# Four first products by quarters beside the modulation, and their loads on another queue

## The chip, the core and the metric

The program runs on one core of a Trainium2 chip, in one launch. A core has a matrix engine (TensorE, here PE, with its weight loads as PEld), a vector engine (VectorE, DVE), a scalar engine (ScalarE, ACT), GpSimd (POOL) and a sync engine (SP) that does little but issue transfers. The metric is the device time of one execution in microseconds; lower is better. The time before is 2888.81 us, the median of three runs (2887.84 to 2892.58).

## The reference

The model is one inference step of a two-layer backbone over 128 context tokens and 128 latent tokens of width 2048, all in float32. Each layer does, for both groups of tokens with the same weights:

```
sh1, sc1, g1, sh2, sc2, g2 = silu(cond) @ ada_w + ada_b        # six vectors of 2048: the modulation
h = rmsnorm(x, nw0) * (1 + sc1) + sh1
u = h @ w_in            # columns: q, k, v | hyena | r, k, v of RWKV | low-rank decay and rate (w_dn, a_dn) | gate
o = concat(attention, hyena, rwkv) @ w_out
x = x + g1 * rmsnorm(o, nw1)
h = rmsnorm(x, nw2) * (1 + sc2) + sh2
x = x + g2 * rmsnorm(relu(h @ w1)^2 @ w2, nw3)
```

The first product of a layer, `h @ w_in`, needs `sc1` and `sh1`, and these need two sixths of `ada_w`: 33.6 MB of the layer's 100 MB of modulation weights. RWKV is a recurrence over the tokens in both directions; the kernel does it in blocks, with a triangular inverse on the vector engine.

## The kernel before

All products with big weights are done in two parts: a weight tile is loaded as float32 (`wr`, up to 512 KB), the scalar engine rounds it to its high part (`wh`, L232), the vector engine subtracts to get the low part (`wl`, L233), and the matrix engine adds three products: high by high, high by low, low by high (L508, L511, L512 in `ws`; L530, L533, L534 in `as_`). The activations (`acth`, `actl`) are split in the same way by `norm` (L468 to L491), in four chunks of 512 of the 2048 model columns. A chunk is four tiles of 128 of the contraction, so a product can begin on the first chunk before the rest is normalised.

The modulation of layer 0 is the boot. Its shift and scale are done in eight groups, one for each of four chunks and the two vectors (`ada_group`, L334). A group loads eight tiles of 512 KB and multiplies them by silu(cond); its 16 matmuls of 512 columns are 32 instructions in the trace. A group ends with a copy (L353) and small products that turn rows into columns (L357). Two groups run in turn (`ada_boot`, L420). After both groups of a chunk `norm` makes that chunk of the activations.

Weight tiles stand in rings: `wr` has four buffers (`raw=4`), `wa` six (`araw=6`). The groups take `wr` and `wa` by turns, the products take `wr`; all of these loads are issued by SP in one order (L342 and L231). A load into a ring waits until the buffer's last reader is done, and what SP has queued behind it waits too.

`mixer_first` (L1120) starts two products of layer 0, `wa` (the low-rank columns, four blocks of 96) and RWKV's `k` (three blocks of 128). In the boot loop of `build` (L1319) each chunk of `norm` is followed by four contraction tiles of the one and four of the other. Both add up in the two PSUM tiles tagged `mm` (`mm_bufs=2`), so these two are taken through the boot. `mixer` (L1127) then does the gate's product (L1155), and RWKV's `r` and `v` (L1158), and only then puts the recurrence of RWKV (`rwkv_batch`) in the list of side work (L1159). Side work is small work on all engines that `run` (L1109) lays between products at a given rate; the modulation vectors still to come (`ada_vector`, L374) are laid between them in the same way. In layer 1 the mixer has the same order, with no boot.

The instructions of an engine are put in order by a scheduler that works on its own model of durations, so their order can differ from the order of the code.

Of the kernel before, what the change touches and what calls it, by code (L numbers as in the profile page):

```python
# [9 lines left out]
F32 = mybir.dt.float32  # L10
# [8 lines left out]
KT = 16  # L19
# [14 lines left out]
def _shape_constants():  # L34
# [56 lines left out]
    for k, v in c.items():  # L91
# [18 lines left out]
            ni=3, w2=0.5, w3=3, w4=2, w5=0.4, fill=16, b1=2, b2=5)  # L110
# [47 lines left out]
class Kern:  # L158
# [65 lines left out]
    def wload(self, src, nk, ncol):  # L224

        nc = self.nc
# [4 lines left out]
        nc.sync.dma_start(v(raw), src.rearrange("(k p) c -> p k c", p=128))  # L231
# [102 lines left out]
    def ada_group(self, l, P, i, cg):  # L334

        nc, sb, A = self.nc, self.sb, self.A
        ps = self.sm()
        c0 = i * D + cg * 512
        for kq in range(8):
            tag = ("wr", "wa")[kq // 2 % 2]  # L340
# [153 lines left out]
    def ws(self, act, w, widths, ps):  # L494
# [4 lines left out]
        for kq in range(KT // nk):  # L499
            hi, lo = self.wload(w[kq * nk * 128:(kq + 1) * nk * 128, :], nk, ncol)  # L500
            for kk in range(nk):
                k = kq * nk + kk
                hh, hl = act[k // 4][0][:, k % 4, :], act[k // 4][1][:, k % 4, :]
                c0 = 0
                for b, wd in enumerate(widths):
                    o = ps[0:wd, b * 256:(b + 1) * 256]
                    h, lw = hi[:, kk, c0:c0 + wd], lo[:, kk, c0:c0 + wd]
                    m = self.product(nc.tensor.matmul(o, lhsT=h, rhs=hh, start=(k == 0 and b % 2 == 0), stop=False, skip_group_check=True))  # L508
# [3 lines left out]
                    nc.tensor.matmul(o, lhsT=lw, rhs=hh, start=False, stop=(k == KT - 1), skip_group_check=True)  # L512
# [596 lines left out]
    def run(self, gen, side=0, ada=0.0):  # L1109

        for n in gen:
            n /= 6144
# [190 lines left out]
    def build(self):  # L1303
# [8 lines left out]
        n, cg, todo = 0, 0, deque()  # L1312

        def products():
            for _, g in first:
                for _ in range(4):
                    next(g)

        while self.adaq or todo:  # L1319
            if self.adaq:  # L1320
                self.ada_boot()
# [7 lines left out]
            if cg < 4 and len(self.adaq) < 2 * (4 - cg) - 1:  # L1329

                todo.append((n + self.o["b1"], lambda: next(norm)))
                todo.append((n + self.o["b2"], products))
                cg += 1
# [58 lines left out]
```

## Time and profile before

| what | us |
|---|---|
| median of three runs | 2888.81 |
| the profiled execution's own time | 2894.91 |
| its span, first to last instruction | 2893.1 |
| PE busy | 2810.1 (97%) |
| DVE busy | 1646.9 (57%) |
| ACT busy | 1232.4 (43%) |
| POOL busy | 179.4 (6%) |
| bytes moved, mean rate | 654.56 MB, 226 GB/s |

The profiled execution is 6.1 us above the median. Matmuls overlap in the array and their ends are modelled, so a busy PE is not PE at its peak: the pace of products is better read from the starts of successive matmuls than from the busy time. The share of DMA can read slightly over 1.

### The profile page before, as it was taken

To read this page: it belongs to the slowest core of one execution; us is meant where nothing else is said; L and a number is where in the kernel's file an instruction comes from. 1 tells how busy PE (TensorE), PEld (TensorE's weight loads), DVE (VectorE), ACT (ScalarE), POOL (GpSimd) and SP (SyncE) were. 2 spreads that over 40 slices of the span, in tenths; PEclk is the share of its full clock that TensorE was granted. 3 is DMA by queue.
4 is the path that set the end of the run, shared out by engine and by line. 5 is a ranking of instruction groups with operands and counts; after the bars stand their busy time and mean duration, and the time that the engine had idled before them with its cause. 6 is when DMAs were issued, how large, how long until landed. Compare 5 with 4: busy or idle time off the path is not lost. (4 is left out here: it accounts for less than half of the span.)

```text
span 2893.1 us, 47892 instructions
## 1 busy us (share of the span) xinstructions
PE 2810.1 (97%) x19163; PEld 2306.6 (80%) x19163; DVE 1646.9 (57%) x2635; ACT 1232.4 (43%) x1878; POOL 179.4 (6%) x368
## 2 busy tenths in 40 slices
PE   6899999999999999999998999999989999999998
PEld 3586888766797897897876979877669989899896
DVE  1356766777544454444455577677675545555555
ACT  2254445434544343343345454453354444444343
POOL 0012101202000000000000111011010000000000
PEclk8999999999999999999999999999899999999999
DMA  9985675478888787887876746534686666666674
GB/s 333 333 300 201 223 231 161 152 261 285 311 268 268 261 270 256 272 274 262 288 279 210 210 149 193 168 111 142 200 297 184 184 186 185 189 189 183 190 241 150
DMA packets 326185, 654.56 MB, mean 226 GB/s; under 512 B 48709, under 2 KB 86158, under 8 KB 325835
## 3 DMA queue, kind: packets, MB, share of 16 engines
q1 hardware_dynamic: 311456, 610.88, 65.3%
q0 software_dynamic: 12928, 36.98, 3.9%
q10 hardware_dynamic: 1579, 3.64, 0.3%
q8 instruction: 150, 2.46, 0.3%
q14 instruction: 72, 0.59, 0.1%
HBM read 632.21 MB, written 19.20 MB: 225 GB/s over the span
## 5 line engine op out<-in xcount | busy, mean ns | idle before, releaser
L233 DVE TENSOR_TENSOR wl<-wr,wh 128x1024 fp32r<-128x1024 f32 (+2 forms) x792 | 929.0, 1175 | 921.1 <-ACT wh L232 909.6
L232 ACT CAST wh<-wr 128x1024 fp32r<-128x1024 f32 (+2 forms) x792 | 798.7, 1010 | 1175.5 <-PE mm L511 522.6
L508 PE MATMUL mm<-acth,wh 128*128 128x256 f32 (+1 forms) x3200 | 921.2, 288 | 6.5 <-ACT acth L489 4.6
L511 PE MATMUL mm<-actl,wh 128*128 128x256 f32 (+1 forms) x3200 | 904.7, 283 | 0.0
L512 PE MATMUL mm<-acth,wl 128*128 128x256 f32 (+1 forms) x3200 | 902.9, 282 | 1.9 <-DVE wl L233 1.9
L508 PEld LDWEIGHTS mm<-acth,wh 128*128 128x128 f32 (+1 forms) x3200 | 601.8, 188 | 59.2 <-issue 32.1
L512 PEld LDWEIGHTS mm<-acth,wl 128*128 128x128 f32 (+1 forms) x3200 | 602.8, 188 | 7.3 <-DVE wl L233 4.3
L511 PEld LDWEIGHTS mm<-actl,wh 128*128 128x128 f32 (+1 forms) x3200 | 600.9, 188 | 4.5 <-issue 3.3
L530 PE MATMUL mm<-wh,fh 128*128 128x512 f32 x1024 | 404.9, 395 | 0.0
L533 PE MATMUL mm<-wl,fh 128*128 128x512 f32 x1024 | 403.3, 394 | 1.0 <-DVE wl L233 0.9
L534 PE MATMUL mm<-wh,fl 128*128 128x512 f32 x1024 | 401.6, 392 | 0.0
L530 PEld LDWEIGHTS mm<-wh,fh 128*128 128x128 f32 x1024 | 192.2, 188 | 56.6 <-issue 8.4
L533 PEld LDWEIGHTS mm<-wl,fh 128*128 128x128 f32 x1024 | 192.2, 188 | 44.9 <-DVE wl L233 2.7
L534 PEld LDWEIGHTS mm<-wh,fl 128*128 128x128 f32 x1024 | 192.0, 187 | 45.2
L387 PE MATMUL ada<-wa,cs 128*32 128x512 f32 x1280 | 193.3, 609 | 8.4 <-DMA wa<-in_ada_w_dram 8.4
L530 PE MATMUL mm<-wh,osh 128*128 128x512 f32 x256 | 106.9, 418 | 0.7 <-ACT osh L1192 0.7
L387 PEld LDWEIGHTS ada<-wa,cs 128*32 128x32 f32 x1280 | 36.6, 109 | 85.9 <-issue 53.6
L533 PE MATMUL mm<-wl,osh 128*128 128x512 f32 x256 | 103.1, 403 | 1.5 <-DVE wl L233 1.5
L534 PE MATMUL mm<-wh,osl 128*128 128x512 f32 x256 | 102.8, 402 | 0.0
L921 PE MATMUL sm<-rZR,rKB 64*128 64x256 f32 x384 | 75.1, 424 | 1.0 <-DVE rLA L925 1.0
L530 PE MATMUL mm<-wh,acth 128*128 128x512 f32 (+1 forms) x192 | 74.3, 387 | 0.0
L533 PE MATMUL mm<-wl,acth 128*128 128x512 f32 (+1 forms) x192 | 68.8, 358 | 0.0
(323 smaller groups left out, 2565.4 us busy)
## 6 DMA issues: line engine op xcount, KB each, us to landing
wr<-in_mlp_w_dram SPq DMA_DIRECT2D x512, 512.0 KB
wa<-in_ada_w_dram SPq DMA_DIRECT2D x352, 512.0 KB
wr<-in_w_in_dram SPq DMA_DIRECT2D x96, 512.0 KB
wr<-in_w_in_dram SPq DMA_DIRECT2D x112, 384.0 KB
wr<-in_w_out_dram SPq DMA_DIRECT2D x56, 512.0 KB
wr<-in_ada_w_dram SPq DMA_DIRECT2D x32, 512.0 KB
gb<-gate POOLq DMA_DIRECT2D x16, 512.0 KB, 8.7
xd<-acc SPq DMA_DIRECT2D x24, 256.0 KB
```

The costliest lines, as they stand in the source:

```text
L232: nc.scalar.copy(hi, raw)
L233: nc.vector.tensor_sub(lo, raw, hi)
L387: nc.tensor.matmul(ps[32 * j:32 * j + 32, :], lhsT=self.cs[:, kk, :], rhs=w[2 * (kk - k + 1) + j // 2][:, 512 * (j % 2):512 * (j % 2) + 51 ...
L508: m = self.product(nc.tensor.matmul(o, lhsT=h, rhs=hh, start=(k == 0 and b % 2 == 0), stop=False, skip_group_check=True))
L511: nc.tensor.matmul(o, lhsT=h, rhs=hl, start=False, stop=False, skip_group_check=True)
L512: nc.tensor.matmul(o, lhsT=lw, rhs=hh, start=False, stop=(k == KT - 1), skip_group_check=True)
L530: m = self.product(nc.tensor.matmul(o, lhsT=hh, rhs=hi[:, kk, :], start=first, stop=False))
L533: nc.tensor.matmul(o, lhsT=hh, rhs=lo[:, kk, :], start=False, stop=False)
L534: nc.tensor.matmul(o, lhsT=hl, rhs=hi[:, kk, :], start=False, stop=last)
L921: self.beside(nc.tensor.matmul(ps[h][:, i * 256:(i + 1) * 256], lhsT=KB[hs, d, g, i, :], rhs=ZR[hs, d, g, :, :].rearrange("p i t -> p (i t ...
```

## The change

1. `mixer_first` is now one generator. It goes through the four chunks of the contraction, and in each through four products: `wa`, `k`, `r` and `v`. Each quarter of a product takes a PSUM tile of its own, and is then copied (first chunk, ACT) or added (later chunks, DVE) to a float32 tile in SBUF (`F`). `ws` takes the range of contraction tiles, `ks`.
2. The loads of these 32 weight tiles are issued by GpSimd (`q=nc.gpsimd`), not by SP.
3. In `ada_group` only the first chunk's groups use the `wr` ring; the later ones use `wa` alone (L340).
4. The boot loop lays 1.2 steps of the modulation (`bo`) beside each contraction tile of the products, for the next chunk's groups.
5. In `mixer` layer 0 finishes the last chunk, takes the convolutions from `F`, adds the recurrence to the side work, and then does the gate's product. Layer 1 does `wa`, then `k`, `r`, `v`, then adds the recurrence, then the gate.

```diff
-            tag = ("wr", "wa")[kq // 2 % 2]
+            tag = "wa" if cg > 0 else ("wr", "wa")[kq // 2 % 2]
...
-        nc.sync.dma_start(v(raw), src.rearrange("(k p) c -> p k c", p=128))
+        (q or nc.sync).dma_start(v(raw), src.rearrange("(k p) c -> p k c", p=128))
...
     def mixer_first(self, l, act):
 
+
+        nc, sb = self.nc, self.sb
         W = self.A["w_in"][l]
-        ps = self.mm(), self.mm()
-        return [(ps[0], self.ws(act, W[:, C_WA:C_WA + 384], [96] * 4, ps[0])),
-                (ps[1], self.ws(act, W[:, C_R + 768:C_R + 768 + 384], [128] * 3, ps[1]))]
+        F = self.F = {n: sb([128, 1024], F32, tag="f" + n) for n in ("wa", "k", "r", "v")}
+        cols = {"wa": (C_WA, [96] * 4), "k": (C_R + 768, [128] * 3), "r": (C_R, [128] * 3), "v": (C_R + 1536, [128] * 3)}
+        for c in range(4):
+            for n, (c0, widths) in cols.items():
+                ps = self.mm()
+                yield from self.ws(act, W[:, c0:c0 + sum(widths)], widths, ps, range(4 * c, 4 * c + 4), nc.gpsimd)
+                dst, src = (x[0:widths[0], 0:256 * len(widths)] for x in (F[n], ps))
+                if c == 0:
+                    nc.scalar.copy(dst, src)
+                else:
+                    nc.vector.tensor_add(dst, dst, src)
+            yield None
...
-        self.run(first[0][1], 1, ada)
-        self.rwkv_lora(first[0][0], P)
-        self.run(first[1][1], 1, ada)
-        rkv_conv("k", 0, first[1][0])
+        if first is not None:
+
+            self.run(first, 1, ada)
+            self.rwkv_lora(self.F["wa"], P)
+            for nm in "krv":
+                rkv_conv(nm, 0, self.F[nm])
+        else:
+            ps = self.mm()
+            self.run(self.ws(act, W[:, C_WA:C_WA + 384], [96] * 4, ps), 1, ada)
+            self.rwkv_lora(ps, P)
+            rkv(0)
+        self.side.add(self.rwkv_batch(l, P, 0, u), self.rwkv_out(l, P, 0), self.rwkv_batch(l, P, 1, u), self.rwkv_out(l, P, 1))
         ps = self.mm()
         self.run(self.ws(act, W[:, C_G:C_G + 256], [128] * 2, ps), o["sh"], ada)
         self.rwkv_gate(ps, P)
-
-        rkv(0, "rv")
-        self.side.add(self.rwkv_batch(l, P, 0, u), self.rwkv_out(l, P, 0), self.rwkv_batch(l, P, 1, u), self.rwkv_out(l, P, 1))
...
+        for c in range(4):
+
+            next(norm)
+            if c < 3:
+                left, due = 2 * (2 - c), 0.0
+                for step in iter(lambda: next(first), None):
+                    due += self.o["bo"]
+                    while due >= 1 and len(self.adaq) > left:
+                        self.ada_boot()
+                        due -= 1
+                while len(self.adaq) > left:
+                    self.ada_boot()
```

What this does to the order, at three places. The first is PE at the end of the second chunk's groups, before: `sm_245` and `sm_248` are the groups' sums, `sm_475` and `sm_478` those of the next chunk, `sm_489` and `sm_503` the transposed activations, `mm_111` is `wa`.

```order
L357 MATMUL sm_245<-const_66,arow_459 128x2 x4
L348 MATMUL sm_248<-wa_453,cs_71 32x512 x2
L357 MATMUL sm_248<-const_66,arow_461 128x2 x4
L348 MATMUL sm_475<-wr_476,cs_71 32x512 x2
L479 MATMUL sm_489<-const_66,xn_487 128x128 x4
L479 MATMUL sm_503<-const_66,xn_501 128x128 x4
L348 MATMUL sm_475<-wr_481,cs_71 32x512 x2
L348 MATMUL sm_478<-wr_479,cs_71 32x512 x2
L348 MATMUL sm_478<-wr_515,cs_71 32x512 x2
L348 MATMUL sm_475<-wa_521,cs_71 32x512 x2
L348 MATMUL sm_478<-wa_523,cs_71 32x512 x2
L508 MATMUL mm_111<-acth_105,wh_526 96x256
```

The same place now; `mm_509` is the quarter of `v`, `sm_243` and `sm_309` are the groups' sums.

```order
L512 MATMUL mm_509<-acth_103,wl_544 128x256
L357 MATMUL sm_243<-const_66,arow_540 128x2 x4
L357 MATMUL sm_309<-const_66,arow_557 128x2 x4
L479 MATMUL sm_586<-const_66,xn_584 128x128 x4
L479 MATMUL sm_600<-const_66,xn_598 128x128 x4
L348 MATMUL sm_581<-wa_582,cs_71 32x512 x2
L348 MATMUL sm_581<-wa_646,cs_71 32x512 x2
L348 MATMUL sm_631<-wa_632,cs_71 32x512 x2
L348 MATMUL sm_631<-wa_670,cs_71 32x512 x2
L348 MATMUL sm_581<-wa_688,cs_71 32x512 x2
L348 MATMUL sm_631<-wa_707,cs_71 32x512
L508 MATMUL mm_612<-acth_105,wh_614 96x256
```

The groups' last matmuls have moved among the products of the chunk before, and the products now stand right ahead of the small products of L357; what lies between L357 and the next chunk's first product has stayed much the same. The second place is the loads: SP before, at the first chunk's products.

```order
L231 DMA wr_367<-in_w_in_dram 128x2x384
L231 DMA wr_391<-in_w_in_dram 128x2x384
L342 DMA wa_415<-in_ada_w_dram 128x2x512
L342 DMA wa_421<-in_ada_w_dram 128x2x512
L342 DMA wr_427<-in_ada_w_dram 128x2x512
L342 DMA wr_429<-in_ada_w_dram 128x2x512
```

POOL now, from its beginning, with what each load waits for.

```order
L307 DMA psink_7340<-in_attn_sink_dram 128x12
L231 DMA wr_291<-in_w_in_dram 128x2x384 [waits DMAHW3_49,DMAHW1_49,PE_49]
L231 DMA wr_330<-in_w_in_dram 128x2x384 [waits DMAHW6_49,DMAHW4_49,PE_49]
L231 DMA wr_370<-in_w_in_dram 128x2x384 [waits DMAHW6_49,DMAHW5_49,PE_49]
L231 DMA wr_408<-in_w_in_dram 128x2x384 [waits DMAHW2_49,DMAHW0_49,PE_49]
L231 DMA wr_438<-in_w_in_dram 128x2x384 [waits DMASW1_49,DVE_49]
```

The weight tiles have left SP's queue and stand alone on POOL's, where from the fifth on each waits for DVE's subtraction on the tile four before it. The third place is far from the boot: PE in the second half of layer 0's recurrence (L1019 and L1021, the block steps that need each other), before; `mm_6216` is a product of `w_out`.

```order
L534 MATMUL mm_6216<-wh_6344,osl_5688 128x512
L530 MATMUL mm_6216<-wh_6344,osh_5687 128x512
L533 MATMUL mm_6216<-wl_6345,osh_5687 128x512
L534 MATMUL mm_6216<-wh_6344,osl_5688 128x512
L1021 MATMUL sm_6355<-rG_4911,rXT_6163 32x64 x8
L1021 MATMUL sm_6356<-rG_5221,rXT_6163 32x64 x8
L1021 MATMUL sm_6357<-rG_5498,rXT_6163 32x64 x8
L387 MATMUL ada_4855<-wa_6388,cs_71 32x512 x2
L530 MATMUL mm_6216<-wh_6344,osh_5687 128x512
```

The same steps now.

```order
L1019 MATMUL sm_6165<-rG_5277,rLA_5274 32x64
L1021 MATMUL sm_6232<-rG_4665,rXT_6024 32x64 x8
L387 MATMUL ada_5524<-wa_6467,cs_71 32x512
L1021 MATMUL sm_6233<-rG_4988,rXT_6024 32x64 x8
L1021 MATMUL sm_6234<-rG_5277,rXT_6024 32x64 x8
L387 MATMUL ada_5524<-wa_6467,cs_71 32x512
L1019 MATMUL sm_6297<-rG_4665,rLA_4661 32x64
L1019 MATMUL sm_6297<-rG_4665,rLA_4662 32x64
```

In this half of the recurrence 90 products of 512 columns stood between the first and the last L1021 before, and 108 up to L1038, which follows; now it is 30 and 48. In layer 1 it was 77 up to L1038 and is 48.

## Rows read from the trace of the kernel before

**Rows 1.** The page: busy time of PE, and two lines of the 40 slices.
```profile
PE 2810.1 (97%) x19163; PEld 2306.6 (80%) x19163; DVE 1646.9 (57%) x2635; ACT 1232.4 (43%) x1878; POOL 179.4 (6%) x368
...
PE   6899999999999999999998999999989999999998
...
GB/s 333 333 300 201 223 231 161 152 261 285 311 268 268 261 270 256 272 274 262 288 279 210 210 149 193 168 111 142 200 297 184 184 186 185 189 189 183 190 241 150
```

**Rows 2.** Busy time by stretch: PE, PEld, DVE, ACT, POOL, PE's clock, DMA, GB/s.
```profile
100.00:120.00 20.00, 19.08 (x134) 12.84 (x131) 7.08 (x11) 6.10 (x10) 0.00 (x0) 0.92 0.90 321
120.00:140.00 20.00, 15.01 (x78) 8.59 (x73) 6.55 (x14) 6.21 (x11) 3.20 (x6) 0.76 0.86 305
```

**Rows 3.** The same for L508 alone, to the end of the boot.
```profile
0.00:134.00 134.00, 24.50 (x84) 15.19 (x84) 0.90 0.93 334
```

**Rows 4.** Waits of SP's queue, 0 to 300 us: total us, times, longest.
```profile
SPq L342 <- DVE wl L233: 15.8, 12, 3.7
SPq L342 <- PE sm L348: 12.0, 9, 4.6
```

**Rows 5.** The boot in order of time: start us, us, instruction, [idle before].
```profile
47.93 0.62 ACT L489 CAST acth<-xnt 128x512 fp32r<-128x512 f32 x1 [0.72 <-DVE xnt L487]
...
50.27 0.36 PE L508 MATMUL mm<-acth,wh 128*96 128x256 f32 x1 [1.26 <-ACT wh L232]
...
84.66 0.29 PE L508 MATMUL mm<-acth,wh 128*128 128x256 f32 x1
...
87.02 0.28 PE L512 MATMUL mm<-acth,wl 128*128 128x256 f32 x1
...
89.02 0.62 PE L348 MATMUL sm<-wa,cs 128*32 128x512 f32 x2
...
90.33 0.60 PE L348 MATMUL sm<-wa,cs 128*32 128x512 f32 x2
...
127.81 1.05 PE L357 MATMUL sm<-const,arow 128*128 128x2 f32 x8 [0.41 <-ACT arow L353]
...
134.90 0.74 PE L508 MATMUL mm<-acth,wh 128*96 128x256 f32 x2 [3.04 <-ACT acth L489]
...
136.16 0.41 PE L508 MATMUL mm<-acth,wh 128*96 128x256 f32 x1
...
140.64 0.37 PE L508 MATMUL mm<-acth,wh 128*96 128x256 f32 x1
```

**Rows 6.** Layer 0 after the boot: the convolution after `v`, and two groups of small products.
```profile
208.32 0.47 ACT L543 ACTIVATE ru_v<-mm,pv 128x256 f32<-128x256 f32 x1
...
L609 PE MATMUL sm<-hhs,const 128*128 128x512 f32 x4 | 2.0, 591 | 0.0
L596 PE MATMUL sm<-hf,hh 64*128 64x512 f32 x4 | 2.0, 615 | 0.0
```

**Rows 7.** GpSimd's transfers: an issue beside DVE's work, and the median time to landing.
```profile
508.98 0.72 POOL L201 DMA_DIRECT2D rup<-in_rw_w_up_dram  x1
509.14 0.43 DVE L852 TENSOR_SCALAR rth<-rth 128x516 f32<-128x516 f32 x1
...
xo<-xd POOLq DMA_DIRECT2D x12, 512.0 KB, 13.8
```

**Rows 8.** The second half of the recurrence in layer 0, and one stretch of layer 1.
```profile
632.97 0.52 PE L1021 MATMUL sm<-rG,rXT 32*32 32x64 f32 x6
634.39 1.52 PE L1021 MATMUL sm<-rG,rXT 32*32 32x64 f32 x42
635.93 1.09 PE L1019 MATMUL sm<-rG,rLA 128*32 128x64 f32 x32
...
672.77 1.53 PE L1021 MATMUL sm<-rG,rXT 32*32 32x64 f32 x48
...
L530 PE MATMUL mm<-wh,osh 128*128 128x512 f32 x31 | 12.8, 417 | 0.0
...
2060.00:2065.00 5.00, 4.91 (x60) 3.93 (x60) 1.61 (x4) 1.10 (x3) 0.00 (x0) 0.50 0.98 345
```

More of the change, by code (lines that the diff above doesn't have):

```diff
@@ L109 @@
             ada_mlp=(0.6, 0.1), sr=3.5, sq=3, sh=4, so=7, ra=0.3, wa1=1.5, wa2=0.5, w0=1, w1=3, wi=0.5,
-            ni=3, w2=0.5, w3=3, w4=2, w5=0.4, fill=16, b1=2, b2=5)
+            ni=3, w2=0.5, w3=3, w4=2, w5=0.4, fill=16, bo=1.2)
 class Pools:
@@ L222, in split, with wload @@
         return hi, lo
-    def wload(self, src, nk, ncol):
+    def wload(self, src, nk, ncol, q=None):
         nc = self.nc
@@ L491, in norm, with ws @@
             yield
-    def ws(self, act, w, widths, ps):
+    def ws(self, act, w, widths, ps, ks=range(KT), q=None):
         nc = self.nc
@@ L498, in ws @@
         nk = 2 if ncol > 256 else 4
-        for kq in range(KT // nk):
-            hi, lo = self.wload(w[kq * nk * 128:(kq + 1) * nk * 128, :], nk, ncol)
+        for k0 in ks[::nk]:
+            hi, lo = self.wload(w[k0 * 128:(k0 + nk) * 128, :], nk, ncol, q)
             for kk in range(nk):
-                k = kq * nk + kk
+                k = k0 + kk
                 hh, hl = act[k // 4][0][:, k % 4, :], act[k // 4][1][:, k % 4, :]
@@ L507, in ws @@
                     h, lw = hi[:, kk, c0:c0 + wd], lo[:, kk, c0:c0 + wd]
-                    m = self.product(nc.tensor.matmul(o, lhsT=h, rhs=hh, start=(k == 0 and b % 2 == 0), stop=False, skip_group_check=True))
+                    m = self.product(nc.tensor.matmul(o, lhsT=h, rhs=hh, start=(k == ks[0] and b % 2 == 0), stop=False, skip_group_check=True))
                     if b == 0 and kk == 0:
@@ L511, in ws @@
                     nc.tensor.matmul(o, lhsT=h, rhs=hl, start=False, stop=False, skip_group_check=True)
-                    nc.tensor.matmul(o, lhsT=lw, rhs=hh, start=False, stop=(k == KT - 1), skip_group_check=True)
+                    nc.tensor.matmul(o, lhsT=lw, rhs=hh, start=False, stop=(k == ks[-1]), skip_group_check=True)
                     c0 += wd
@@ L1111, in run @@
         for n in gen:
-            n /= 6144
+            n = (n or 0) / 6144
             self.side.now += n
@@ L1311, in build @@
         first = self.mixer_first(0, act)
[L1312 to L1321, printed above, removed]
+        n = 0
+        while len(self.adaq) > 6:
+            self.ada_boot()
             n += 1
@@ L1328, in build @@
                 norm = self.norm(P[0], next(rest), 1, 0, act)
[L1329 to L1333, printed above, removed]
-            while todo and (todo[0][0] <= n or not self.adaq):
-                todo.popleft()[1]()
+        for c in range(4):
[8 more added lines that the diff above has]
+                while len(self.adaq) > left:
+                    self.ada_boot()
         for l in range(DEPTH):
@@ L1344, in build @@
                     pass
-                first = self.mixer_first(l, act)
-            acc, ss = self.mixer(l, p, act, first)
+            acc, ss = self.mixer(l, p, act, first if l == 0 else None)
             self.ada_until(l, 3)
```

## The prediction

> **What bounds the kernel now.** I read the page first, then the stretches, then the boot in order of time. PE is busy for 2810.1 of 2893.1 us, and of the 40 slices of 72.3 us the first two stand lowest or near it, at six and eight tenths, where almost all others have nine [rows 1]. So a change that leaves PE's work as it is can give only what PE idles or waits for, and the place to look is the boot. The busy time hides some of it: successive products of 256 columns start 0.118 us apart (84.66 to 87.02 us, 20 steps), yet each is drawn as 0.28 us [rows 5]. By pace the 84 products of a chunk need 9.9 us, and the 64 instructions of two modulation groups 7.0 us (from 89.02 to 90.33 us 12 began, those on `wr` tiles counted, 0.109 us each) [rows 5]. A chunk lasted some 28 us: its first products start at 50.27 us in the first, at 134.90 us in the fourth, so 28.2 us each [rows 5]. With L357 (2.1 us) PE has some 9 us of slack a chunk, and it is spent on transfers (321 and 305 GB/s at a DMA share of 0.90 and 0.86 [rows 2]) and on the chain from the groups' end to the next products.
>
> **What moves.** Per chunk `r` and `v` add 72 products, 72 x 0.118 = 8.5 us; over the first three chunks 25.5 us of PE work goes from behind the boot into it. What I price is how much later the fourth chunk's products begin, against 134.90 us.
>
> *First products.* The activations of the first chunk were ready at 48.55 us, the products waited for their weights to 50.27 us [rows 5]. Now those tiles are asked for earlier, when the first groups let go of `wr`. They then compete with the last modulation tiles; the four hold 1.57 MB, 4.7 us at 334 GB/s [rows 3]. Bounds 49 to 54 us; I take 51, near the row. Some 27 of the first products will run at the half clock again, as after the idle stretch at 130 us, where 21 of them took 4.48 us, 0.213 us each, before the clock rose [rows 5]: 27 x 0.095 = 2.6 us.
>
> *A chunk.* The order now puts the products right ahead of L357, then the transposes, 12 instructions of the next groups, and the next chunk's first product. 156 products at 0.118 = 18.4 us; the other 52 modulation instructions 5.7 us; L357 twice 1.05 = 2.1 us; and from the end of L357 to the first product 6.0 us, as from 128.9 to 134.90 us [rows 5]. That chain stays, and only the 12 instructions lie in it. Together 32.2 us if nothing waits for a transfer.
>
> *Transfers.* A chunk has 16 modulation tiles, 8.4 MB, and 8 weight tiles, 3.1 MB: 11.5 MB in 32.2 us is 358 GB/s, a little over the 334 that the boot had on average [rows 3]. SP no longer holds modulation loads behind a product's `wr` buffers (12 waits, 15.8 us [rows 4]), so I expect a higher rate, but not one without waits: 1.8 us a chunk, 34 us. Bounds: none (32.2) to 38 us (11.5 MB at 305 GB/s [rows 2]). The fourth chunk then begins at 51 + 2.6 + 3 x 34 = 155.6 us. By bytes: 44.8 MB before 134 us [rows 3], and 4.7 MB of `r` and `v` and four more tiles of the later modulation (2.1 MB), which the order puts ahead, make 51.6 MB, 332 GB/s by then: the two agree.
>
> The Trainium skill (DMA: Bandwidth & Descriptors, Issuing engines are not separate DMA queues) says that transfers issued by several engines run on the same 16 DMA engines and interleave, and that issuing from several saves only the sequencer's time. By that rule alone the rate would stay 334 GB/s and the fourth chunk would begin at 51.6 / 0.334 = 154.5 us, about my sum; no run here shows yet what the second queue does.
>
> *Evictions.* 4 copies on ACT and 12 additions on DVE are new. ACT takes 0.47 us for 256 columns out of PSUM [rows 6], so 1.4 to 1.9 us each; DVE had 7.1 of 20 us busy [rows 2]. Each has the next quarter's 36 products (4.2 us) to hide behind, because PSUM has two such tiles: nothing. Without that cover it would be 16 x 1.6 = 26 us.
>
> *After the boot.* From 134.90 us the old order ran the last 84 products, the gate, `r` and `v`, and ended at 208.32 us [rows 6]. The new one runs 156 products (18.4 us), the gate's 96 (11.3), 32 instructions of the later modulation (3.5), the Hyena filter's small products (four L596 at 2.0 and six L609 at 3.0, 5 us [rows 6]), and I add 3 us of waits and 1.3 us of half clock: 42.5 us, so to 198.1 us. It has then done 16 modulation instructions more than the old one at 208.32 us (1.7 us), so it is ahead by 208.3 + 1.7 - 198.1 = 11.9 us.
>
> *The recurrence, later.* The scheduler has moved its second half against the products of `w_out`: 30 of these stand among the steps where 90 stood. From 632.97 to 672.77 us, 39.8 us, PE did 91 products (31 of them L530 [rows 8]) at twice 0.118 us, 21.5 us. The 60 that left the stretch are still done, but their 14.2 us no longer cover the waits between steps. If all of it turned into waiting the cost would be 14 us; but L1019 began at 635.93 us, 0.02 us after the L1021 before it ended, with no product between [rows 8], so the steps overlap among blocks. I take 3 us, near that row, for both layers; bounds 0 to 14 in layer 0, and as layer 1 shows the half clock after such a wait (0.50 at 2060 us [rows 8]), up to 5 more there. The earlier start of the side work in both layers changes no instruction; I cost it at nothing, since products run beside it.
>
> *Sum.* 11.9 - 3 = 8.9 us. The profiled execution of 2894.91 us (span 2893.1 us and 1.8 around it) would become 2886.0 us; it lies 6.1 us above the median, so against the median I forecast 2888.8 - 8.9 = 2879.9, say 2880 us.
>
> **Rivals.**
>
> *The boot is bound by transfers.* For it: DMA shares of 0.86 to 0.90 and 305 GB/s in its last stretch [rows 2]. Against it: SP waited 15.8 us behind `wr` [rows 4], which ends. At 320 GB/s the fourth chunk begins at 51.6 / 0.32 = 161 us, 5.6 us later than I say: gain 3.3 us, 2885 us. Chance 0.22.
>
> *The weight tiles come too late from GpSimd: slower.* Four buffers turn, each after issue (0.72 us [rows 7]), landing, rounding and subtraction (1.8 us). With a landing of 13.8 us, as for the slowest of GpSimd's big loads [rows 7], a tile comes every 16.3 / 4 = 4.1 us, eight in 32.6 us: just hidden. The point of decision is a chunk of 37 us, 4.6 us a tile, a landing of 16 us. At 18 us a chunk takes 41 us, the fourth begins at 177 us, and the run loses 9 us there and 3 later: 2901 us. Against it: 13.8 was measured among other traffic, and the loads are asked for four tiles ahead. Chance 0.08.
>
> Here the Trainium skill (SBUF — State Buffer, Who interferes with whom) says that GpSimd cannot write its transfers' descriptors while DVE runs certain copies and scalar operations at double rate. The nearest row has such a scalar operation beside an issue, 0.43 us of it within 0.72 us [rows 7]; if each of 32 issues grew by as much, it would be 14 us of GpSimd's idle time and nothing on PE's path.
>
> *The recurrence pays for the lost cover: slower.* With 14 us in layer 0 and 5 in layer 1 the gain of 11.9 turns into a loss of 7 us: 2896 us. It decides from 12 us on. Against it: the 0.02 us of [rows 8]. Chance 0.08.
>
> *More than forecast.* No waits for transfers, first products at 49 us and a recurrence that costs nothing: the fourth chunk at 49 + 2.6 + 96.6 = 148 us, gain 11.9 + 7.4 = 19.3 us, 2869 us. Chance 0.15.
>
> **How the numbers follow.** My case has 0.47, with a range of its own of 2874 to 2886 us. A difference of 0.2%, 5.8 us, is about what a measurement can tell from none. Faster: four fifths of my case, the best case and a quarter of the transfer case, 0.38 + 0.15 + 0.05 = 0.58. Slower: the two slower rivals but 0.02, 0.14. The rest, 0.28, is the same. The range goes from 2863 us (the best case with the first half clock gone and its spread) to 2896 us (a recurrence at its bound; the late tiles beyond).
>
> **What would show it.** Right: first products of the fourth chunk at 150 to 160 us; chunks of 32 to 36 us; SP's L342 no longer waiting for DVE; the gate's product ending near 198 us; landing of GpSimd's weight tiles under 13 us; the second half of layer 0's recurrence shorter than 39.8 us, with 30 products in it, by less than their 14 us. Wrong: a chunk of over 37 us, PE waiting for ACT's rounding of a GpSimd tile, an addition into `F` that PE waits for, or a stall of PE at L1019 or L1021.

## The result, and the profile after

The changed kernel takes 2922.21 us (median of four runs, 2918.56 to 2932.11) against 2888.32 us for the old one beside it: a ratio of 1.0121, 95% interval 1.0092 to 1.0150. It is 34 us slower, where 9 us faster was forecast and the range ended at 2896 us. The profiled execution took 2925.24 us, with a span of 2923.5 us and 1.7 us around it; the old span was 2893.1, so the two traces differ by 30.4 us.

The page of the kernel after, its lines that answer to [rows 1]:

```profile
PE 2825.0 (97%) x19163; PEld 2307.0 (79%) x19163; DVE 1660.0 (57%) x2647; ACT 1236.6 (42%) x1882; POOL 202.0 (7%) x400
...
PE   6989999999999999999998999999989999999998
...
GB/s 341 324 281 130 237 228 161 137 238 290 323 258 278 259 260 277 256 261 255 287 317 219 205 115 217 186 79 143 207 296 188 187 185 185 188 189 185 191 239 151
```

The second slice rose from eight tenths to nine and the third fell from nine to eight: the idle time moved and did not go. In the fourth slice, 219 to 292 us, transfers fell from 201 to 130 GB/s. Busy time by stretch shows where, first of the kernel after and then of the kernel before (columns as in [rows 2]):

```profile
20.00:50.00 30.00, 18.08 (x75) 4.75 (x73) 5.87 (x17) 13.04 (x31) 4.26 (x6) 0.72 1.04 406
50.00:120.00 70.00, 65.44 (x492) 46.85 (x492) 27.76 (x44) 24.43 (x36) 12.17 (x18) 0.97 0.94 347
120.00:150.00 30.00, 30.00 (x210) 20.33 (x203) 10.65 (x13) 7.63 (x10) 6.36 (x10) 0.96 0.85 300
150.00:180.00 30.00, 27.61 (x187) 20.86 (x187) 14.45 (x30) 14.94 (x23) 4.73 (x8) 0.89 0.87 310
180.00:210.00 30.00, 24.66 (x161) 16.28 (x160) 17.83 (x31) 13.65 (x23) 8.90 (x15) 1.00 0.82 275
210.00:270.00 60.00, 57.69 (x282) 41.13 (x282) 43.15 (x85) 28.29 (x51) 6.76 (x17) 0.97 0.33 108
```

```profile
20.00:50.00 30.00, 20.96 (x87) 5.63 (x85) 5.11 (x16) 11.96 (x29) 0.00 (x0) 0.72 1.03 390
50.00:120.00 70.00, 63.73 (x446) 42.84 (x447) 19.80 (x34) 17.29 (x28) 0.00 (x0) 0.95 0.98 351
120.00:150.00 30.00, 25.01 (x157) 18.28 (x152) 9.73 (x17) 13.37 (x20) 4.61 (x8) 0.83 0.90 309
150.00:180.00 30.00, 29.98 (x219) 24.07 (x220) 18.30 (x33) 15.62 (x23) 2.19 (x4) 1.00 0.72 225
180.00:210.00 30.00, 30.00 (x242) 25.78 (x235) 14.29 (x18) 11.32 (x15) 6.08 (x10) 1.00 0.98 341
210.00:270.00 60.00, 59.23 (x293) 39.23 (x292) 41.60 (x78) 30.47 (x56) 10.49 (x24) 1.00 0.63 219
```

To 150 us the change does what it was made for: 702 PE instructions from 50 to 150 us against 603. Then it turns: PE idles 7.7 of 60 us from 150 to 210 us, where the old kernel was busy throughout, and from 210 to 270 us it asks for half the old rate of transfers, with DVE busier: PE does more side work there than the old kernel (159 instructions against 132), fewer products and no modulation. By bytes (rate times time) both kernels had moved the same from 20 to 210 us, 63.0 and 62.5 MB. The boot had little to spare but PE time, and the products of `r` and `v` brought their 4.7 MB with them.

For the rest of the run I weighted each PE instruction with the mean time from its start to the next one's in the old trace (outliers cut at 1.5 times the median), and read off when each kernel had done the same sum of work. The column is the time of the kernel after less that of the kernel before, and beside it the same for two of the experiments below. The row at 166 us hangs on how the outliers are cut, by 5 us and more; the others move by 1 to 2 us. Each column is one execution, and that of f1 lies 7 us above its median:

```
old kernel at us    after   f1      e11     where the old kernel is
 144                -15.2   -12.2   -15.3   fourth chunk's products
 166                 -7.4    -0.1    -7.7   gate done, r begins
 188                 -4.2    +2.1    -5.6   v begins
 211                 +4.4    +6.4    -1.1   q, k, v begin
 346                 +8.9   +10.4    +2.6   second part of k, r, v
 510                +11.4   +12.0    +2.4   Hyena products
 534                +23.1   +13.2    -0.1   the same
 768                +20.1   +14.6    +0.3   MLP of layer 0
1583                +23.5   +16.6    +0.2   mixer of layer 1
2197                +30.7   +25.3    +7.1   MLP of layer 1, to the end
```

So the boot was up to 15 us ahead, and 20 were lost by the time that the old kernel had the gate, `r` and `v` done; 12 more went between 510 and 534 us, 3 of which came back; 7 went in layer 1's mixer. Three groups of rows stand for these. First, two rows of the order of time on PE (as in [rows 5]), one of ACT, and PE's waits from 150 to 222 us:

```profile
50.38 0.48 PE L508 MATMUL mm<-acth,wh 128*96 128x256 f32 x2
...
158.71 0.48 PE L508 MATMUL mm<-acth,wh 128*96 128x256 f32 x2
...
219.91 0.58 ACT L778 ACTIVATE rsg<-mm 128x512 f32<-128x512 f32 x1
```

```profile
PE ada L387 <- DMA wa<-in_ada_w_dram: 4.9, 4, 2.3
PE sm L800 <- DMA rs<-in_state_rwkv_dram: 2.9, 1, 2.9
```

A chunk took (158.71 - 50.38) / 3 = 36.1 us, and the gate, whose product L778 reads at 219.91 us (the old kernel's `v` was read at 208.32 [rows 6]), came 61.2 us after the fourth chunk's first product. L800 is a first step of the recurrence; it now stands ahead of the gate, and PE waited 2.9 us for its state to land. Next SP's waits from 50 to 160 us, answering [rows 4]:

```profile
SPq L342 <- PE sm L348: 69.6, 26, 8.9
SPq L382 <- PE ada L387: 7.2, 2, 5.7
```

In this stretch SP's modulation loads no longer wait for DVE's `wl`, as forecast. They wait for PE to empty the modulation's ring instead, 69.6 us. Last, the start of the second batch of the recurrence in layer 0, in order of time on PE, and a stretch behind it:

```profile
505.18 0.44 PE L897 MATMUL sm<-const,rkf 128*128 128x128 f32 x2 [1.85 <-ACT rkf L891]
...
534.58 0.44 PE L897 MATMUL sm<-const,rkf 128*128 128x128 f32 x2 [2.82 <-ACT rkf L891]
```

```profile
535.00:555.00 20.00, 20.00 (x68) 11.55 (x66) 10.97 (x26) 5.64 (x15) 0.75 (x1) 0.52 0.20 57
```

PE waited 2.82 us for ACT's `rkf`, and from then to 555 us it ran at the lower level, a granted clock of 0.52 with 68 instructions in 20 us.

### The profile page after: what moved, and what is told of

It is laid out like the page before. It is cut to its first block, busy times and chain, and to the rows that moved or that the text cites. A ratio compares the mean times of both kernels' runs of the same rounds, so it can differ in the third digit from the quotient of the medians.

```text
span 2923.5 us, 47956 instructions
## 1 busy us (share of the span) xinstructions
PE 2825.0 (97%) x19163; PEld 2307.0 (79%) x19163; DVE 1660.0 (57%) x2647; ACT 1236.6 (42%) x1882; POOL 202.0 (7%) x400
## 5 line engine op out<-in xcount | busy, mean ns | idle before, releaser
L508 PE MATMUL mm<-acth,wh 128*128 128x256 f32 (+1 forms) x3200 | 922.1, 288 | 2.2 <-ACT acth L489 2.0
L508 PEld LDWEIGHTS mm<-acth,wh 128*128 128x128 f32 (+1 forms) x3200 | 600.5, 188 | 63.1 <-issue 37.1
L512 PEld LDWEIGHTS mm<-acth,wl 128*128 128x128 f32 (+1 forms) x3200 | 602.3, 188 | 11.5 <-issue 4.9
L511 PEld LDWEIGHTS mm<-actl,wh 128*128 128x128 f32 (+1 forms) x3200 | 600.1, 188 | 11.5 <-issue 8.2
L530 PEld LDWEIGHTS mm<-wh,fh 128*128 128x128 f32 x1024 | 192.4, 188 | 61.2 <-issue 8.4
L921 PE MATMUL sm<-rZR,rKB 64*128 64x256 f32 x384 | 87.1, 432 | 1.2 <-DVE rLA L925 0.8
```

What stands on the lines that cost most here:

```text
L511: nc.tensor.matmul(o, lhsT=h, rhs=hl, start=False, stop=False, skip_group_check=True)
L530: m = self.product(nc.tensor.matmul(o, lhsT=hh, rhs=hi[:, kk, :], start=first, stop=False))
L921: self.beside(nc.tensor.matmul(ps[h][:, i * 256:(i + 1) * 256], lhsT=KB[hs, d, g, i, :], rhs=ZR[hs, d, g, :, :].rearrange("p i t -> p (i t ...
```

## The experiments

Ratios are to runs of the old kernel on the same chip, with 95% intervals.

**Order of layer 1 (e1): 1.0084 [1.0055, 1.0113], 2916.95 us.**

```
-            rkv(0)
-        self.side.add(self.rwkv_batch(l, P, 0, u), ...)
+            rkv(0, "k")
+        if first is not None:
+            self.side.add(self.rwkv_batch(l, P, 0, u), ...)
...
         self.rwkv_gate(ps, P)
+        if first is None:
+            rkv(0, "rv")
+            self.side.add(self.rwkv_batch(l, P, 0, u), ...)
```

> The changed kernel with layer 1's mixer in the old order (wa, k, gate, r, v, then the recurrence's side work); layer 0 as changed. The changed kernel loses 30 us of span against the old one: 24 us stand by the end of layer 0's mixer, some 7 us more come in layer 1's. Theory A (the new order of the mixer costs time in layer 1 as well, since side work that starts before the gate crowds its products): about 2915 us, and layer 1's loss against the old trace is under 2 us. Rival (layer 1's loss is where stalls of the recurrence happen to fall, with no lasting sign): 2922 us give or take 4.

It came out between the two, nearer to theory A. The ratio suggests 0.4%, some 10 us, for layer 1's order, but its interval overlaps that of the kernel after, and the one trace (19 us above the median) has a longer layer 1, with other stretches at the lower clock. What the traces do agree on is PE's idle time in that mixer, 14.3 us here against 20.0, as told under the prediction's steps below. The old order is not quite restored: beside layer 1's `k` the side work keeps rate 3.5, where the old kernel had 1. That holds for e2, e3, e4, e10 and e11 too, which share this order of layer 1.

**Side work behind layer 0's gate, first try (e2): 1.0107 [1.0075, 1.0140], 2926.18 us.**

```
-        self.side.add(self.rwkv_batch(l, P, 0, u), ...)
...
         self.rwkv_gate(ps, P)
+        self.side.add(self.rwkv_batch(l, P, 0, u), ...)
...
-            self.run(self.as_(lhs, range(KT), W[:, c0:c0 + n], n, ps), o["sq"], ada)
+            self.run(self.as_(lhs, range(KT), W[:, c0:c0 + n], n, ps), 4 if first is not None else o["sq"], ada)
```

> As e1, and in layer 0 too the recurrence's side work is queued only after the gate's products (with a side rate of 4 in place of 3 in the q, k, v products behind it, so that its buffers turn). The products of r and v stay in the boot. Theory A (side work that starts ahead of the gate takes its place on DVE, and with its loads on the transfers): the gate ends near 208 us in place of 219.9, the wait of 2.9 us for the state's load is off the path, and the stall at 530 us with its half clock does not come: 2895 us. Theory B (the boot's own tail is the cause: modulation tiles arrive late, the clock falls): the gate still ends at 214 us or later, 2908 us or more.

No gain, but the gate was done at 211.1 us in place of 219.9 and the wait at L800 was gone. What undid it is not shown. At the higher rate the recurrence's first blocks stood 62 and 92 products of 256 columns apart (96 and 106 in the kernel after), and 20.5 us at the lower clock followed at 295 us; but f1, below, has its blocks 66 and 86 apart and gains. The rate is the likely cause: b1 and b5, below, differ by it (and in buffers), and b1 is 18 us the slower. Three changes are in this run (layer 1's order, the side work's place, the rate); f1 leaves layer 1 as changed and takes a rate of 3.5.

**No later modulation asked for beside the fourth chunk and the gate (e3): 1.0102 [1.0073, 1.0131], 2924.06 us.**

```
-            self.run(first, 1, ada)
+            self.run(first, 1, 0.0)
...
-        self.run(self.ws(act, W[:, C_G:C_G + 256], [128] * 2, ps), o["sh"], ada)
+        self.run(self.ws(act, W[:, C_G:C_G + 256], [128] * 2, ps), o["sh"], 0.0 if first is not None else ada)
```

> As e1, and no later modulation is put beside layer 0's fourth quarter and its gate; its groups run later. Theory B (PE waits 7.2 us for modulation tiles there, which SP asks for only once the gate's weight tiles ahead of them in its queue have a buffer): these waits go, the half clock at 160 us too, the gate ends at or before 208 us, and 5 to 10 us of the run are gained, 2905 to 2910 us. Theory A (the crowd of side work on DVE sets this stretch): the gate's 4.4 us of modulation go from the stretch and little else; the products wait for their weights' rounding instead, 2913 us or more.

The edit did not bring about its condition: PE still had the same 32 modulation instructions in a row at 188.6 us, since the scheduler drew later ones forward. Theory B is not tried by it.

**wa and k alone by quarters (e4): 1.0067 [1.0031, 1.0102], 2906.94 us.**

```
-        F = self.F = {n: sb([128, 1024], F32, tag="f" + n) for n in ("wa", "k", "r", "v")}
+        F = self.F = {n: sb([128, 1024], F32, tag="f" + n) for n in ("wa", "k")}
...
         self.rwkv_gate(ps, P)
+        rkv(0, "rv")
+        self.side.add(self.rwkv_batch(l, P, 0, u), ...)
```

> The new boot for the two products that the old one had there (wa and k) by quarters, with GpSimd's loads, the sums in SBUF and the modulation's own ring; r and v come after the gate as in the old kernel, and the side work's order is the old one in both layers. Theory A (the order of r, v and side work is at fault, the boot's mechanics are sound): the old kernel's time or better, 2880 to 2890 us. Rival C (GpSimd's loads, the additions on DVE or the one ring are at fault): 2900 us or more, with the loss before 210 us.

It came out as rival C had it: over 2900 us, with some 22 us of the loss there by 210 us. With the old order and the old amount of PE work in the boot, the boot's mechanics cost 0.7%: the fourth chunk began at 157.5 us, 22.6 us later than of old.

**The ring alone (p1): 1.0041 [1.0028, 1.0054], 2903.24 us. Ring and GpSimd's loads (p3): 1.0066 [1.0044, 1.0088], 2910.34 us.** Both are the old kernel with:

```
-            tag = ("wr", "wa")[kq // 2 % 2]
+            tag = "wa" if cg > 0 else ("wr", "wa")[kq // 2 % 2]
```

p3 loads the weights of wa and k from GpSimd's queue besides.

> The old kernel with one part of the change alone: the boot's modulation groups, but for the first two, keep to their own ring of six tiles; first products, loads on SP and order as of old. If the ring is harmless, as the prediction had it (SP no longer waits behind wr): 2875 to 2888 us, the boot's modulation (L348) no slower than 69 us of PE's time and the gate done by 180 us. If six tiles are too few to keep the transfers busy: the boot's chunks get longer than 28 us and the run takes 2895 us or more.

> The same with the first two products' weights loaded from GpSimd's queue besides. Sound mechanics: 2870 to 2888 us. Rival C (loads from GpSimd come late or take transfers from the modulation): the boot ends later than with the ring alone, by 5 us or more, and the run takes 2895 us or more.

The fourth chunk began at 155.7 and 163.6 us, against 134.9. The ring alone does it; its stretch and SP's first wait, 50 to 156 us:

```profile
50.00:120.00 70.00, 59.30 (x336) 34.03 (x336) 15.45 (x29) 13.92 (x23) 0.00 (x0) 0.83 0.78 282
```

```profile
SPq L342 <- PE sm L348: 63.2, 26, 10.2
```

With six tiles in turn in place of ten, SP waits for PE and PE for transfers; the DMA engines are busy 0.78 of the time, not 0.98, and move 282 GB/s, not 351. GpSimd's loads add another 7 us there (2910.34 less 2903.24; the two intervals overlap, but the fourth chunk too began 7.9 us later).

**The changed kernel with SP's loads (e7): 1.0142 [1.0124, 1.0160], 2931.69 us; with the old rings (e8): 1.0190 [1.0159, 1.0221], 2942.20 us.**

```
-                yield from self.ws(act, W[:, c0:c0 + sum(widths)], widths, ps, range(4 * c, 4 * c + 4), nc.gpsimd)
+                yield from self.ws(act, W[:, c0:c0 + sum(widths)], widths, ps, range(4 * c, 4 * c + 4))
```

(e7; e8 takes back the line of `tag` that p1 has.)

> The changed kernel with the four first products' weights loaded from SP, as of old, and not from GpSimd. Prediction's view (a queue of their own keeps products and modulation from waiting for each other): slower than the changed kernel by 5 us or more, a chunk over 37 us. Rival C (GpSimd's loads are at fault): chunks of 33 us or less and 2915 us or less.

> The changed kernel with the boot's modulation on the two old rings (six wa and four wr tiles by turns), all else as changed. The ring alone had cost the old boot 22 us. Theory D (six tiles hold too little in flight, and in the changed boot the products of r and v only fill what PE waits for modulation tiles): the fourth chunk's products begin at 151 us or earlier in place of 158.7, and the run takes 2910 to 2916 us. Rival (the changed boot is bound by PE's products and the chain between chunks, so tiles in time change nothing, or products wait behind wr again): 156 to 162 us, 2919 us or more.

In the changed boot both parts help, the ring clearly (e8), GpSimd's loads by the boot of the one trace: the interval of e7 overlaps that of the kernel after. From 50 to 120 us, e7 first and then e8:

```profile
50.00:120.00 70.00, 67.79 (x430) 44.46 (x431) 20.72 (x31) 18.76 (x28) 0.00 (x0) 0.95 0.82 297
```

```profile
50.00:120.00 70.00, 62.66 (x422) 44.39 (x422) 21.32 (x33) 20.39 (x29) 10.24 (x15) 0.93 0.92 326
```

In the kernel after it is 347 GB/s, and 326 to 342 in the seven other kernels with its boot. The fourth chunk began at 169.3 us (e7) and 173.7 us (e8; 174.3 in e10, with the same rings), not at 158.7 (158.4 to 166.0 in those seven). In e8 GpSimd stood 59 us behind PE's modulation before it could load into `wr`:

```profile
POOL wr L231 <- PE sm L348: 59.0, 11, 10.8
```

So theory D fell for the changed boot. As I read it, the products' tiles, always in flight on a queue of their own, fill there the place of the four tiles that the old boot lost.

**The gate's weights from GpSimd (e5): 1.0117 [1.0101, 1.0133], 2924.28 us.**

```
-  self.ws(act, W[:, C_G:C_G + 256], [128] * 2, ps)
+  self.ws(act, W[:, C_G:C_G + 256], [128] * 2, ps, q=nc.gpsimd if l == 0 else None)
```

> The changed kernel, with the weights of layer 0's gate loaded from GpSimd's queue too, so that on SP nothing stands ahead of the later modulation's tiles between the boot and the q, k, v products. Theory B (in the changed kernel SP issues none of these tiles from 162.8 to 187.5 us, because the gate's fifth weight tile waits for a buffer): the wait of 2.3 us at 188 us and the burst of transfers after it go, the state's load lands before it is needed, and the gate ends at 213 us or earlier in place of 219.9; the run gains 4 to 7 us, 2916 us. Rival (the tiles come late because the transfers are full): the gate ends within 2 us of 219.9, 2922 us.

The gate's product was read at 228.7 us, 63.1 us after the fourth chunk's start. PE's waits for modulation tiles stayed (158 to 230 us), and SP now waits for PE's use of that ring, up to 23 us at a time, with nothing ahead of it:

```profile
PE ada L387 <- DMA wa<-in_ada_w_dram: 5.7, 4, 2.7
```

```profile
SPq L382 <- PE ada L387: 34.5, 6, 23.2
```

Theory B falls: what stands ahead in SP's queue is not what holds these tiles. 32 instructions in a row use eight tiles, the ring holds six, and the last two are asked for only when the first have been used.

**Wider spacing of the second batch (e9): 1.0121 [1.0106, 1.0136], 2922.74 us.**

```
-            self.run(self.ws(act, W[:, c0:c0 + 512], [128] * 4, ps), o["sh"], ada)
+            self.run(self.ws(act, W[:, c0:c0 + 512], [128] * 4, ps), 3 if l == 0 else o["sh"], ada)
```

> The changed kernel with the side work beside layer 0's Hyena products at rate 3 in place of 4. By the order the recurrence's second batch then has 106 and 84 products between its three blocks where 59 and 83 stand. Theory E (with the blocks so near one another PE runs out of products and waits 2 to 3 us for the next block's first transposes, L897 for ACT's rkf, and the clock halves behind it): the waits at 505 and 534 us fall to under 2 us, the half clock of 20.5 us at 535 us goes, layer 0 gains 8 to 12 us, 2911 to 2914 us. Rival (the waits are luck of one execution): no change beyond 4 us, 2918 to 2926 us, and a half-clock stretch of like length elsewhere in layer 0.

The two waits and the lower clock behind them went; layer 0's mixer ended 6.5 us earlier (the first transposes of its MLP's norm, L479, at 739.7 us in place of 746.2). But one wait of 7.0 us came in their place (480 to 620 us), and the median did not move:

```profile
PE mm L533 <- DVE wl L233: 7.0, 1, 7.0
```

**All three (e10): 1.0144 [1.0121, 1.0168], 2930.48 us.** Its edits are those of e8, e9 and e1.

> Old ring in the boot, side rate 3 beside layer 0's Hyena products, and layer 1's mixer in the old order, in the changed kernel. If the boot's ring (D), the second batch's spacing (E) and layer 1's order each cost what the traces suggest (6 to 8, 8 to 12 and some 6 us), 2896 to 2902 us; what is then left over the old kernel is the wait in the fourth quarter and the gate. If they don't add up: 2910 us or more.

They don't add up, since the old rings cost the changed boot.

**The order alone, in the old kernel (b1): 1.0213 [1.0194, 1.0233], 2950.83 us; at the old rate, with other buffers (b5): 1.0146 [1.0111, 1.0180], 2932.71 us. r and v first, side work where it was (b4): 0.9995 [0.9980, 1.0010], 2887.34 us.**

```
+        rkv(0, "rv")
+        self.side.add(self.rwkv_batch(l, P, 0, u), ...)
...
         self.rwkv_gate(ps, P)
-        rkv(0, "rv")
-        self.side.add(self.rwkv_batch(l, P, 0, u), ...)
```

(b4 moves the first line alone; b1 has rate 4 in place of 3 beside layer 0's q, k, v, and b5 `k1=23, k2=14, k4=19` in place of 25, 15 and 18.)

> The old kernel, boot and all, with the mixer's order alone changed in both layers: r and v ahead of the gate, and the recurrence's side work queued before the gate (side rate 4 beside layer 0's q, k, v products, so that its buffers turn). Theory A (the order costs, whatever the boot): the boot as of old to 160 us, then 10 us lost in layer 0's mixer and some 6 in layer 1's, 2900 to 2906 us. Rival (only together with the new boot does it cost): 2883 to 2892 us.

> As the run of the order alone (r and v, then the recurrence's side work, then the gate, both layers, old boot), but at the old side rate of 3 beside the q, k, v products; for its buffers one 4 KB tile more and a few small ones less (k4 19, k1 23, k2 14). That run was 62 us over the old kernel, 41 of it in layer 0's mixer. Theory A (starting the side work before the gate puts its steps closer to one another than PE's products can cover): still 15 to 40 us over the old kernel, 2903 to 2928 us, with L921 (the products behind which PE waits in the recurrence) 6 us or more longer in layer 0. Rival (the rate of 4 was at fault there): 2884 to 2894 us.

> The old kernel with one thing moved: in both layers the products of r and v stand ahead of the gate's. The recurrence's side work is still queued after the gate; boot, rings and rates as of old. If r and v ahead of the gate cost nothing (the cost is the side work's earlier start, theory A): 2884 to 2892 us. If the nine convolutions that then come together on DVE, or the weights' order, are at fault: 2897 us or more, with the loss before 240 us.

With the old boot, moving `r` and `v` ahead of the gate costs nothing (b4), and queueing the recurrence's side work ahead of it costs 1.5% (b5). What b5's other buffers cost by themselves was not tried. Both b1 and b5 lost more than theory A had forecast (2900 to 2906 and 2903 to 2928 us). By the weights of the table above, b5 lost 6 us in layer 0 behind the boot and 27 in layer 1's mixer, b1, at the rate of 4, 42 and 15. L921 took 4.5 us more in b5's layer 0 than in b4's, where 6 or more were expected, and 9.3 more in layer 1. b5 and then b4, the recurrence's L921 in layer 1 (1500 to 2200 us; busy, mean ns of one):

```profile
L921 PE MATMUL sm<-rZR,rKB 64*128 64x256 f32 x192 | 47.5, 472 | 0.6 <-DVE ast L732 0.4
```

```profile
L921 PE MATMUL sm<-rZR,rKB 64*128 64x256 f32 x192 | 38.2, 429 | 0.0
```

**The side work in layer 0 behind the gate (f1): 1.0078 [1.0056, 1.0099], 2912.69 us. With rate 3 beside Hyena and layer 1's old order as well (e11): 1.0036 [1.0022, 1.0049], 2901.83 us.**

```
-        self.side.add(self.rwkv_batch(l, P, 0, u), ...)
+        if first is None:
+            self.side.add(self.rwkv_batch(l, P, 0, u), ...)
...
         self.rwkv_gate(ps, P)
+        if first is not None:
+            self.side.add(self.rwkv_batch(l, P, 0, u), ...)
...
-            self.run(self.as_(lhs, range(KT), W[:, c0:c0 + n], n, ps), o["sq"], ada)
+            self.run(self.as_(lhs, range(KT), W[:, c0:c0 + n], n, ps), 3.5 if first is not None else o["sq"], ada)
```

> The changed kernel with one thing undone: in layer 0 the recurrence's side work is queued after the gate and not before it (side rate 3.5 in place of 3 beside q, k, v, so that its buffers turn). Layer 1 and the Hyena products' rate are as changed. Theory A alone (the earlier start in layer 0 costs): layer 0's mixer ends 10 to 17 us earlier than in the changed kernel, the wait for the state's load is gone, 2906 to 2912 us; the rest over the old kernel is layer 1's order and the boot's tail. Rival (the two other edits of the run before, rate 3 and layer 1's old order, gave the 20 us there): 2917 us or more.

> The changed kernel with the recurrence's side work queued after layer 0's gate (side rate 3.5 beside q, k, v), side rate 3 beside the Hyena products, layer 1 in the old order. Theory A and E together: the boot stays as it is (4 us ahead of the old kernel at equal work by 188 us), and the 14 us of the second batch's waits and the 7 of layer 1 go: 2890 to 2900 us. Rival (the loss sits in the boot's tail and in r and v being loaded within it, not in the side work's place): 2910 us or more.

Both came just above the ranges of theories A and A with E. From 1.0121 to 1.0078 is 0.43%, 12 us, for the side work's place in layer 0, with the rate of 3.5 that its buffers need (the two intervals still touch; b4 and b5 are far apart). From there to 1.0036 is another 12 us, for layer 1's order and rate 3 beside Hyena together. Their shares are not shown: the rate alone gave nothing in e9's median, but by the table the two traces part by 16 us ahead of layer 1's mixer and by 2 in it, and the fourth chunk began 7.6 us later in f1's trace, after the same instructions. 0.36%, 10 us, is left over the old kernel; the table does not put it in the boot, since e11 is level with the old trace at 768 us and loses 7 us in layer 1's mixer. In the table the kernel after loses 24.3 us from 188 to 768 us, f1 12.5 and e11 5.9. PE's waits in layer 0 from 208 us on, after and e11:

```profile
PE sm L897 <- ACT rkf L891: 6.7, 4, 2.8
```

```profile
PE sm L897 <- ACT rkf L891: 3.6, 4, 2.3
```

**The old kernel with the rate (b3): 0.9986 [0.9969, 1.0003], 2885.89 us; with r and v first too (f2): 0.9994 [0.9978, 1.0010], 2890.94 us.** The edits are those of e9 and b4.

> The old kernel with side rate 3 beside layer 0's Hyena products. In the changed kernel this took 6 us from layer 0's mixer in the profile, and nothing that the medians tell. Theory E (the recurrence's blocks of the second batch need some 100 products between them): they get 111 and 130 in place of 74 and 69, the wait of 1.85 us at 546 us and the half clock behind it go, 2880 to 2885 us. Rival (the side work that is pushed back holds up the output's products): 2890 us or more.

> A version made from what the runs show: the old kernel and its boot, r and v ahead of the gate, the side work queued after it, side rate 3 beside layer 0's Hyena products. The parts alone gave ratios of 0.9995 and 0.9986. If they add up: 2883 to 2887 us, at or just under the old kernel, a difference near what a measurement can tell. If the r and v order undoes the rate's gain: 2888 to 2892 us.

Neither can be told from the old kernel; no version that I ran beats it.

## Why the prediction was wrong

- *"The earlier start of the side work in both layers changes no instruction; I cost it at nothing, since products run beside it."* This step failed most. By the medians the earlier start costs 12 us in layer 0 (f1) and some 10 in layer 1 (e1, whose interval overlaps), and 43 us in the old kernel (b5, both layers, other buffers). Products do run beside it, but not without waits. In layer 0 the time from the fourth chunk's first product to ACT's reading of the gate is 58.7 to 63.1 us in the eight kernels with the changed boot, or a variant of it, that queue the side work ahead of the gate, and 48.4 to 48.6 us in the three that have `r` and `v` in the boot and queue it behind (e2, e11, f1). In layer 1's mixer PE stood idle for 20.0 us where the old kernel idled 12.7, the stretch less the busy time in these rows of after and before (from the last L479 of the norm ahead of it to the first of the MLP's norm):

```profile
1588.46:2175.65 587.19, 567.17 (x4231) 460.81 (x4229) 414.07 (x840) 274.62 (x520) 70.35 (x146) 0.98 0.56 176
```

```profile
1564.93:2146.62 581.69, 569.03 (x4235) 463.13 (x4233) 411.81 (x840) 275.07 (x520) 70.66 (x146) 0.97 0.57 177
```

The same time is 20.0 to 25.7 us in all eight kernels with the side work ahead of the gate in layer 1, and 11.5 to 15.5 us in the twelve with it behind. One wait that all eight have, and none of the twelve above 0.2 us, is that of a product of `w_out` for ACT's rounding of its weights, 2.9 us in the kernel after and 2.6 to 5.2 us over the eight:

```profile
PE mm L530 <- ACT wh L232: 2.9, 1, 2.9
```

What makes up the 12 us of layer 0 stays open. Too few products between the chain's blocks it is not: counted in the traces, 48 and 53 products of 512 columns stood between the first three blocks in the kernel after and 33 and 43 in f1, which is the faster. The clock differs from trace to trace besides, as the stretch at 535 us shows, and e9 took two waits away and another came.
- *Transfers: a higher rate, since SP no longer waits behind `wr`; 34 us a chunk, the fourth at 155.6 us.* The wait went, the rate did not rise: 338 GB/s to 159 us (the row below answers [rows 3]), and 0.338 x 159 = 53.7 MB by then where I had 51.6. The first products began at 50.38 us (51 forecast), without the 2.6 us of half clock; a chunk took 36.1 us, and the fourth began at 158.7 us here and at 158.4 to 166.0 us in the seven other kernels with this boot. I had also left out that six tiles hold less in flight than ten. In the old boot that costs 20.8 us (p1: 155.7 against 134.9); in the changed one the ten tiles shared with the products were the slower way (e8), so it does not explain these 3 us.

```profile
0.00:159.00 159.00, 45.43 (x158) 28.11 (x158) 0.92 0.93 338
```

- *After the boot, 42.5 us to the gate's end.* Measured 61.2; with the side work behind the gate 48.6 (e11: 158.4 to 207.0 us; f1 the same). So some 12.6 us are side work and its wait; the 6 us that are left I put, without a run for it, to modulation instructions that wait for tiles (some 4 us) and a longer stretch at the lower clock. Of the 11.9 us ahead nothing remained: at the old kernel's 211 us the kernel after was 4.4 us behind, and e11 1.1 ahead.
- *The recurrence's lost cover, -3 us.* Sized too high, by the one trace: from 644.40 to 669.47 us the second half took 25.1 us where it had taken 41.3 ([rows 8], each to the end of the last L1021), 16 less with 60 products fewer, whose time is 14 us. No long stall took their place; PE waited 0.61 and 1.05 us at L1019.

```profile
644.40 0.52 PE L1021 MATMUL sm<-rG,rXT 32*32 32x64 f32 x6
...
667.94 1.53 PE L1021 MATMUL sm<-rG,rXT 32*32 32x64 f32 x48
```

- *Evictions at nothing; GpSimd's tiles in time.* Both held: PE waited for no addition into `F`, and the 32 tiles landed in a median of 6.0 us ([rows 7] had 13.8 for bigger loads).

```profile
wr<-in_w_in_dram POOLq DMA_DIRECT2D x32, 384.0 KB, 6.0
```

Of the rivals, the transfer-bound boot (161 us) was nearest for the boot, but no rival had the side work's place in it. The Trainium skill (DMA: Bandwidth & Descriptors, Issuing engines are not separate DMA queues) says that issuing from several engines saves only the sequencer's time. The rate to the fourth chunk agrees: 334 GB/s before, 338 after. But e7, with all of the boot's weight loads on SP, had 305 to its fourth chunk (0 to 169 us). As I read it, loads that wait for a buffer no longer hold up those behind them in SP's order: in e7 the products' loads waited some 18 us there (L231, 50 to 175 us). In the old boot with six tiles the second queue gave only 4 GB/s (p1 282, p3 286).

## What to carry to other kernels

Work brought forward brings its bytes: before moving products into a stretch where PE idles, ask whether the transfers there have room, by their share of time and by the bytes that each version must have moved by the stretch's end. An order of side work is not free because its instructions stay the same: try the reorder by itself first (b4 and b5 would have told it before the boot was rebuilt), and compare PE's idle time over the whole stretch and several traces, not one wait. A count of the products between the chain's steps did not tell it here. Splitting one ring in two can take tiles in flight from both (p1), unless both are always in use (the changed boot).

## What I had not expected of the hardware

The boot's loads, most of them of 512 KB, ran at 351 GB/s from 50 to 120 us with ten tiles in turn and at 282 with six (p1), the DMA engines idle a fifth of the time. After PE's wait of 2.82 us at 532 us the granted clock stayed at the lower level, 1.2 GHz, for some 20 us in which PE did 68 instructions; after the 1.85 us at 505 us no such stretch came in this trace. In e1's trace the wait at 507 us was 2.2 us, and 0.50 was granted from there to 520 us. And the boot varies by 7.6 us between kernels whose instructions on PE are the same, in the same order, through the fourth chunk (158.4 to 166.0 us at the fourth chunk, one trace each), so a boot is compared over several traces.
